# Attention on one core: low parts of the turned weights on GpSimd, and VectorE's scans with an operand in PSUM

## The chip, the cores and the metric

The kernel runs on one core of one Trainium2 chip. The metric is the device time in microseconds of one execution. The engines of the core are TensorE (PE in the profile, with its weight loads as PEld), VectorE (DVE), ScalarE (ACT), GpSimd (POOL) and SyncE (SP), whose queue issues nearly all DMAs. Each engine works through its own instructions in order; semaphores hold an instruction until those that it depends on are done.

## The reference

A decoder trunk of two layers on 1024 positions of width 1024: an RG-LRU block, a feed-forward block, an attention block, a second feed-forward block, and a last norm. The edit lies in the attention, which has 16 heads of 64. In the reference (cut):

```python
z = jnp.einsum("bhqd,bhkd->bhqk", qb, kb).astype(jnp.float32) * scale
strict = s_idx < t_idx
log_fail = jnp.where(strict, jax.nn.log_sigmoid(-z), 0.0)
suffix = lax.cumsum(log_fail, axis=3, reverse=True) - log_fail
weights = jnp.where(strict, jnp.exp(jax.nn.log_sigmoid(z) + suffix), 0.0)
outs.append(jnp.einsum("bhqk,bhkd->bhqd", weights.astype(vb.dtype), vb))
```

Each weight is the chance sigmoid(z) of a position times the product of sigmoid(-z) over the positions between it and the query.

## The kernel before

**How the weights are made.** Let F be sigmoid(-z). The product of F from a position up to the query is what one reversed multiplicative scan along the row gives. The kernel computes these products in place of the weights and moves the difference of neighbouring products onto the values, which are stored as differences of neighbouring rows (L2013). So, for each chunk of 128 queries by up to 512 keys:

- TensorE makes the scores in a PSUM bank (`z_part`, L2091 and L2092, two banks in turn).
- ScalarE writes F = sigmoid of them as float32 into SBUF (`z_rest`, L2129).
- VectorE scans F in place, from right to left (`scan`). A chunk on the diagonal (L2136) multiplies by F and adds `unit`, a row of zeros that ends in a scaled identity block, which starts each row's product at its own diagonal element. A chunk to the left of it (L2139) starts from the first column of the diagonal chunk; its second tensor operand is not used in the arithmetic (`bypass`), and F itself stands there.
- The float32 product is split into two float16 parts in the tile `wx` (four buffers): ScalarE casts the high part (`turn_weights`, L2151) and VectorE subtracts it from F for the low part (L2152).
- One DMA from SyncE's queue (L2161) turns both parts, so that keys lie on the partitions, into `wd`, `wt` or `wp`.
- TensorE multiplies the turned parts by the values (`av_part`, L2203).

In the last of the eight pairs of heads (`q == LAST`) the weights are turned by TensorE instead (`t_part`, L2171) into banks of the pool `psT`, and split from there (`t_split`, L2180 and L2181). `turn_weights` returns at once for that pair. The pool `psT` has two banks, which nothing uses before the last pair.

**The order of work.** Inside `tc.manual_schedule` every engine runs its instructions in the order of the program. Each head has 12 chunks and 12 units of the products with the values. The loop over `u` scores and scans one chunk, splits and turns the chunk of the step before, takes one postponed task from `later`, and issues two steps of `fill`: the projections that make queries, keys and values of the next pair (`qkv_steps`), on TensorE. A chunk's products with the values come about ten steps after its scan. With each chunk of the first seven pairs but the first of a diagonal pair comes a turn, ten for a head, 140 in all: 84 of 512 columns and 56 of 384.

Other work of the stage that shares the queues:

- On VectorE: L1960, low parts of projection weights; L2011 and L2013, values; L2052 and L2066, queries and keys; L2018, low parts of values; L2216, outputs of a head; L2228, low parts of outputs.
- On ScalarE: L1945, squares of weights; L1952, high parts of projection weights; L2041 and L2049, key and query pieces; L2061 and L2074, their casts.
- On GpSimd: L2070, memsets of the unused half of the key tiles `kk`; L1938 to L1941, four small factor instructions; L2220, an addition of values to the output of a pair; L1958, low parts of two weights for the stage that follows.
- On SyncE's queue, beside L2161: L129, loads of weights; L2040 and L2048, copies of key and query pieces to the other half of the partitions; L2022, the turning of the values.

`unit` is made once at the start of the stage by GpSimd (L1896, L1897), in bfloat16. Before the loop, norms are computed by `stats` (square root L205 on ScalarE) and spread over the partitions by TensorE (L216).

Of the kernel before, what the change touches and what calls it, by code (L numbers as in the profile page):

```python
# [8 lines left out]
F32 = mybir.dt.float32  # L9
# [5 lines left out]
ALU = mybir.AluOpType  # L15
# [3 lines left out]
P = 128  # L19
# [4 lines left out]
NB = 512  # L24
# [11 lines left out]
def trunk(  # L36
# [21 lines left out]
    nc = tc.nc  # L58
# [239 lines left out]
    with ExitStack() as st, tc.manual_schedule(engines={E.PE, E.Activation, E.DVE, E.Pool, E.SP}):  # L298
# [95 lines left out]
        for ks in (range(4), range(4, ND)):  # L394
            for lhs, rhs in ((0, xh), (0, xl), (1, xh)):
                for k in ks:
                    first, last = lhs == k == 0 and rhs is xh, lhs == 1 and k == ND - 1
# [1487 lines left out]
    with ExitStack() as st:  # L1885
# [4 lines left out]
        psT = st.enter_context(tc.tile_pool(name="psT", bufs=2, space=PSUM, reuse_waits="tile"))  # L1890
# [4 lines left out]
        unit = ap.tile([P, NB], BF16, name="unit")  # L1895
        nc.gpsimd.memset(unit[:, 0 : NB - P], 0.0)  # L1896
        nc.gpsimd.tensor_scalar_mul(unit[:, NB - P :], ident, UP)  # L1897
        g2 = ap.tile([P, ND], BF16, name="g2")
        nc.scalar.square(g2, vc[:, V_MIX + ND : V_MIX + 2 * ND])
        rs = ap.tile([P, NT], F32, name="rs")  # L1900
# [73 lines left out]
        def qkv_steps(q):  # L1974
            for which in range(3):
                w, at = wq.pop((q, which)), 3 * q + which + 1
                if at < 3 * NP:
                    raw = raws.pop(at)
                    wq[divmod(at, 3)] = next_weights(raw, Q_UP)
                    if which == 1:  # L1980
                        later.extend(column_norms(raw, q))
                else:
                    mix[0].w[mix[0].order[0]] = next_weights(mix[0].raw.pop(0), WO_UP, nc.gpsimd)
                for i in (at + 1,) if at < 3 * NP else (at + 1, at + 2):
                    load_link(i)

                ks = (1, 5, 2, 6, 3, 7, 0, 4) if (q, which) == (0, 0) else range(ND)
                for n in range(NH):
                    pool, tag = (psZ, "z") if (q, which) == (0, 0) else (psQ, "qk")
                    ps = pool.tile([P, NB], F32, tag=tag, name="qk_ps")  # L1990
                    for i, k in enumerate(ks):
                        mm3(ps, w[0][:, k], w[1][:, k], *pair16(xh[k][n]), i == 0, i == ND - 1)
                        if i < ND - 1:
                            yield
                    ev = evacuate(q, which, n, ps)
                    next(ev)
                    yield
                    next(ev, None)
# [102 lines left out]
        LAST = NP - 1  # L2101
# [29 lines left out]
        def scan(q, hx, j, ci, c0, c1, diag):  # L2131
            F = W[q, hx, j, ci]
            n = min(c1, (j + 1) * P) - c0
            rev = F[:, ::-1]
            if diag:
                nc.vector.tensor_tensor_scan(rev, rev, unit[:, NB - n :][:, ::-1], 0.0, op0=ALU.mult, op1=ALU.add)  # L2136
            else:
                first = W[q, hx, j, 1][:, 0:1]
                nc.vector.tensor_tensor_scan(rev, rev, rev, first, op0=ALU.mult, op1=ALU.bypass)  # L2139

        T = {}

        def turn_weights(q, hx, j, ci, c0, c1, diag):
            paired = diag and j % 4 < 2
            if q == LAST or paired and j % 4 == 0:
                return
            F = W[q, hx, j - 1, "pair"] if paired else W[q, hx, j, ci]
            F = F.rearrange("p (b c) -> p b c", c=P)
            m = F.shape[1]
            wx = ap.tile([P, 4, 2, P], F16, tag="wx", name="wx", bufs=4)  # L2150
            nc.scalar.copy(wx[:, 0:m, 0], F)  # L2151
            nc.vector.tensor_sub(wx[:, 0:m, 1], F, wx[:, 0:m, 0])  # L2152
            if paired:
                dst = T[q, hx, j // 4, "pair"] = ap.tile([P, 6, P], F16, tag="wp", name="wp", bufs=2)
            else:
                g = (q, hx, j // 4, diag)
                if g not in T:
                    wide, tag = (2, "wd") if diag else (4, "wt")
                    T[g] = ap.tile([P, 8, wide, P], F16, tag=tag, name=tag, bufs=2)
                dst = T[g][:, 0 : 2 * m, j % 4 - (2 if diag else 0)]  # L2160
            nc.sync.dma_start(dst, wx[:, 0:m].rearrange("p b h c -> p (b h c)"), transpose=True)  # L2161

        def unit_list(q, hx):
            kbs = ((0, 1, 2, 3), (4, 5, 6, 7, 0, 1, 2, 3))
            return [(q, hx, G, kb, kb == 4 * G, kb == 3) for G in range(2) for kb in kbs[G]]
# [70 lines left out]
        units = [u for q, hx in heads for u in unit_list(q, hx)]  # L2236
# [27 lines left out]
        with tc.manual_schedule(engines={E.PE, E.Activation, E.DVE, E.Pool, E.SP}):  # L2264
# [3 lines left out]
            first = qkv_steps(0)  # L2268
# [32 lines left out]
            def turn(some):  # L2301
                for a in some:
                    turn_weights(*a)

            for u in range(-LEAD, len(units)):
# [13 lines left out]
                for a in some:  # L2319
                    scan(*a)  # L2320
# [13 lines left out]
                if u in gains:  # L2334
                    z_rest(z_part(*chunks[c]), *chunks[c])
                    scan(*chunks[c])
                    turning.append(chunks[c])
                    c += 1
# [52 lines left out]
```

## Time and profile before

| what | us |
|---|---|
| median of three runs | 2084.01 |
| lowest and highest of the three | 2081.61 and 2084.85 |
| the profiled execution | 2083.18 |
| its span in the trace | 2081.1 |

Busy time in that execution, by stretches of the span (us from its start): attention proper is the second row, the last pair of heads the third.

| stretch | TensorE | VectorE | ScalarE | GpSimd |
|---|---|---|---|---|
| 940 to 980 | 38.27 | 25.93 | 27.90 | 4.76 |
| 980 to 1340 | 349.19 | 343.48 | 289.97 | 48.90 |
| 1340 to 1385 | 41.08 | 38.97 | 28.59 | 7.56 |

In the rows of a profile, "out<-in" names the tile written and the tiles read, "x" gives the count, and after the bar stand the busy time in us and the mean of one in ns; then, where shown, the idle time of the engine in front of these instructions and what ended it. In rows in order of time, the first number is the start and the second the duration in us; a bracket gives the idle time in front and what ended it. A matmul's row overlaps the next one's, since matmuls are pipelined.

### The profile page before, as it was taken

The page shows a single profiled execution, that of the slowest core. Times are in us where ns is not written, and L with a number is a line of the kernel's source. Part 1 is how long each engine was busy: PE and PEld are TensorE (multiplying, and loading weights), DVE is VectorE, ACT ScalarE, POOL GpSimd, SP SyncE. Part 2 cuts the span into 40 slices and gives each one's busy share as a digit, 9 for nine tenths or more (in the row PEclk, how much of TensorE's full clock was granted, in tenths as well). Part 3 has the DMA queues.
Part 4 walks back from the last instruction along what each step waited for, and adds up shares of the span by engine and source line. Part 5 has one row for each costly group of instructions (what it writes and reads, how often), then busy time and mean ns, then how long its engine had stood idle before and what let it go on. Part 6 is the DMA issues. An engine that isn't in the chain of part 4 may idle for free.

```text
span 2081.1 us, 28578 instructions
## 1 busy us (share of the span) xinstructions
PE 2026.6 (97%) x10059; PEld 1111.7 (53%) x10059; DVE 1847.6 (89%) x2795; ACT 1452.1 (70%) x2279; POOL 116.8 (6%) x154
## 2 busy tenths in 40 slices
PE   8999999999999999999999999999999999999998
PEld 7888885445544444444555555554445545444445
DVE  6887898989898899897999999988899899999886
ACT  6777446777878656566888888755777777665566
POOL 1000010000000000000011111212000000000002
PEclk9999999999999999999999999999999999999999
DMA  7231471675677665233887887754355546674412
GB/s 254 61 97 55 166 222 58 187 231 193 224 228 238 234 219 168 59 101 103 160 157 155 154 153 151 148 175 141 93 195 177 178 153 207 211 257 149 137 46 91
DMA packets 444000, 332.27 MB, mean 160 GB/s; under 512 B 165832, under 2 KB 361552, under 8 KB 443856
## 3 DMA queue, kind: packets, MB, share of 16 engines
q1 hardware_dynamic: 443696, 330.19, 55.0%
q8 instruction: 78, 1.28, 0.3%
q14 instruction: 66, 0.54, 0.1%
q10 hardware_dynamic: 160, 0.27, 0.0%
HBM read 215.55 MB, written 69.21 MB: 137 GB/s over the span
## 4 chain that ended last, share of the span: by engine, by line
PE 59%; DVE 21%; ACT 12%; issue 6%; DMA 2%; SPq 0%; DVEq 0%; ACTq 0%
PE p_ps L158 11%; PE p_ps L156 11%; PE p_ps L157 11%; PE a_ps L157 3%; PE a_ps L158 3%; PE a_ps L156 3%; PE ob_ps L156 2%; PE ob_ps L158 2%; PE ob_ps L157 2%; DVE wx L2152 2%; DVE wa L784 2%; DVE v L1394 2%; ACT kk L2041 1%; ACT w L2129 1%; DVE sb L799 1%
## 5 line engine op out<-in xcount | busy, mean ns | idle before, releaser
L158 PE MATMUL p_ps<-v,wb 128*128 128x512 f16 x524 | 198.8, 379 | 8.1 <-DVE wb L784 7.9
L156 PE MATMUL p_ps<-v,wb 128*128 128x512 f16 x524 | 198.5, 379 | 4.4 <-ACT G L1075 2.6
L158 PE MATMUL p_ps<-v,wc 128*128 128x512 f16 x524 | 198.6, 379 | 3.2 <-DVE wc L784 3.2
L157 PE MATMUL p_ps<-v,wc 128*128 128x512 f16 x524 | 198.6, 379 | 0.0
L157 PE MATMUL p_ps<-v,wb 128*128 128x512 f16 x524 | 198.6, 379 | 0.0
L156 PE MATMUL p_ps<-v,wc 128*128 128x512 f16 x524 | 198.5, 379 | 0.0
L158 PE MATMUL p_ps<-v,wa 128*128 128x512 f16 x396 | 150.1, 379 | 0.0
L157 PE MATMUL p_ps<-v,wa 128*128 128x512 f16 x396 | 150.1, 379 | 0.0
L156 PE MATMUL p_ps<-v,wa 128*128 128x512 f16 x396 | 150.0, 379 | 0.0
L779 ACT ACTIVATE wb<-sb,fac 128x1024 f16<-128x1024 f32 x44 | 50.5, 1148 | 108.8 <-DVE sb L799 108.8
L2151 ACT CAST wx<-w 128x512 f16<-128x512 f32 (+1 forms) x140 | 80.0, 572 | 48.4 <-DVE w L2136 26.4
L156 PE MATMUL p_ps<-v,wd 128*128 128x512 f16 x254 | 96.2, 379 | 6.6 <-ACT G L1486 3.6
L2136 DVE TENSOR_TENSOR_SCAN w<-w,unit 128x128 f32<-128x128 f32 (+1 forms) x112 | 93.4, 834 | 8.8 <-ACT w L2129 7.7
L156 PE MATMUL qk_ps<-rh,w 128*128 128x512 f16 x264 | 101.0, 383 | 0.0
L157 PE MATMUL qk_ps<-rh,w 128*128 128x512 f16 x264 | 100.0, 379 | 0.3 <-DVE rh L250 0.3
L158 PE MATMUL qk_ps<-rh,w 128*128 128x512 f16 x264 | 100.0, 379 | 0.0
L2129 ACT ACTIVATE w<-z_ps,rs 128x512 f32<-128x512 f32 (+2 forms) x168 | 96.4, 577 | 4.6 <-PE z_ps L2092 3.0
L158 PE MATMUL p_ps<-v,wd 128*128 128x512 f16 x254 | 96.3, 379 | 1.5 <-DVE wd L784 1.5
L156 PE MATMUL a_ps<-xh,whi 128*128 128x512 f32 x248 | 97.0, 391 | 0.0
L2091 PE MATMUL z_ps<-kk,q 128*128 128x256 f32 (+1 forms) x192 | 94.1, 490 | 2.9 <-ACT w L2129 1.4
L157 PE MATMUL a_ps<-xl,whi 128*128 128x512 f32 x248 | 96.6, 390 | 0.1
L158 PE MATMUL a_ps<-xh,wlo 128*128 128x512 f32 x248 | 96.6, 389 | 0.0
(489 smaller groups left out, 5591.1 us busy)
## 6 DMA issues: line engine op xcount, KB each, us to landing
raw<-in_ffn_w_in SPq DMA_DIRECT2D x80, 512.0 KB, 4.3
pd<-U SPq DMA_DIRECT2D x90, 256.0 KB, 2.4
loose<-in_ffn_w_out SPq DMA_DIRECT2D x44, 512.0 KB, 4.2
raw<-pd SPq DMA_DIRECT2D x66, 256.0 KB, 3.7
row<-pd SPq DMA_DIRECT2D x62, 256.0 KB, 3.9
raw<-in_ffn_w_out SPq DMA_DIRECT2D x56, 256.0 KB, 3.3
loose<-in_attn_w_qkv SPq DMA_DIRECT2D x24, 512.0 KB, 3.8
raw<-in_attn_w_qkv SPq DMA_DIRECT2D x24, 512.0 KB, 4.6
```

What stands on the lines that cost most here:

```text
L156: nc.tensor.matmul(ps, lhsT=wh, rhs=mh, start=first, stop=False, **kw)
L157: nc.tensor.matmul(ps, lhsT=wh, rhs=ml, start=False, stop=False, **kw)
L158: nc.tensor.matmul(ps, lhsT=wl, rhs=mh, start=False, stop=last, **kw)
L779: nc.scalar.activation(h, r, AF.Copy, scale=up)
L784: V.scalar_tensor_tensor(l, r, up, h, op0=ALU.mult, op1=ALU.subtract)
L799: V.tensor_sub(self.part(self.sb, 0), self.part(self.rb, 0), self.part(self.ra, 0))
L1394: V.scalar_tensor_tensor(lo, raw, power_of(p), hi, op0=ALU.mult, op1=ALU.subtract)
L2091: nc.tensor.matmul(ps[:, 0 : c1 - c0], lhsT=lhsT, rhs=KK[q][hx][:, 0, c0:c1], start=True, stop=False)
L2129: nc.scalar.activation(F, ps[:, 0:n], AF.Sigmoid, scale=rs[:, j : j + 1])
L2136: nc.vector.tensor_tensor_scan(rev, rev, unit[:, NB - n :][:, ::-1], 0.0, op0=ALU.mult, op1=ALU.add)
L2151: nc.scalar.copy(wx[:, 0:m, 0], F)
L2152: nc.vector.tensor_sub(wx[:, 0:m, 1], F, wx[:, 0:m, 0])
```

## The change

The low parts of the turned weights (L2152) are formed by GpSimd. The second tensor operand of the scans in the first seven pairs of heads comes from a PSUM bank, `units_ps`, in which ScalarE writes, once, a reversed float32 copy of `unit`. The bank is the first of the two of `psT`. In the last pair the scans on the diagonal read `unit` in SBUF as before, and those off the diagonal name `unit` in place of F as the operand that is not used.

```diff
         nc.gpsimd.tensor_scalar_mul(unit[:, NB - P :], ident, UP)
+        units_ps = psT.tile([P, NB], F32, tag="T", name="units")
+        nc.scalar.copy(units_ps, unit[:, ::-1])
         g2 = ap.tile([P, ND], BF16, name="g2")
...
             rev = F[:, ::-1]
+            add = unit[:, NB - n :][:, ::-1] if q == LAST else units_ps[:, 0:n]
             if diag:
-                nc.vector.tensor_tensor_scan(rev, rev, unit[:, NB - n :][:, ::-1], 0.0, op0=ALU.mult, op1=ALU.add)
+                nc.vector.tensor_tensor_scan(rev, rev, add, 0.0, op0=ALU.mult, op1=ALU.add)
             else:
                 first = W[q, hx, j, 1][:, 0:1]
-                nc.vector.tensor_tensor_scan(rev, rev, rev, first, op0=ALU.mult, op1=ALU.bypass)
+                nc.vector.tensor_tensor_scan(rev, rev, add, first, op0=ALU.mult, op1=ALU.bypass)
...
             nc.scalar.copy(wx[:, 0:m, 0], F)
-            nc.vector.tensor_sub(wx[:, 0:m, 1], F, wx[:, 0:m, 0])
+            nc.gpsimd.tensor_sub(wx[:, 0:m, 1], F, wx[:, 0:m, 0])
```

## The prediction

> **What bounds the kernel now.** I read the page's engine rows first, then the stage table by stretches of time, then who waits for whom inside the stage that the edit touches, then groups of instructions, then single rows in order of time.
>
> ```profile
> span 2081.1 us, 28578 instructions
> PE 2026.6 (97%) x10059; PEld 1111.7 (53%) x10059; DVE 1847.6 (89%) x2795; ACT 1452.1 (70%) x2279; POOL 116.8 (6%) x154
> ```
>
> Everything edited lies in the attention stage, from about 980 us, when the first chunk is scanned, to 1340 us, when the last head pair, which is not turned by transfers, takes over.
>
> ```profile
> core 0: us, PE busy (x) PEld busy (x) DVE busy (x) ACT busy (x) POOL busy (x), PEclk, DMA share, GB/s
> 980.00:1340.00 360.00, 349.19 (x1864) 187.69 (x1862) 343.48 (x490) 289.97 (x538) 48.90 (x63) 1.00 0.81 156
> ```
>
> In these 360 us VectorE is busy 95%, ScalarE 81%, GpSimd 14%. TensorE's rows leave only 360.00 - 349.19 = 10.8 us idle, at the full clock. So TensorE's own work is the floor, and the change can bring back only what TensorE waits. These are its waits, and those of the engines that make it wait:
>
> ```profile
> ACT wx L2151 <- DVE w L2136: 26.4, 26, 2.4
> ACT wx L2151 <- DVE w L2139: 19.4, 23, 1.8
> PEld z_ps L2091 <- ACT w L2129: 9.5, 18, 0.9
> PE av_ps L2203 <- DMA wt<-wx: 3.6, 5, 1.0
> PE n_ps L1927 <- ACT sq L1945: 3.0, 6, 0.7
> PE z_ps L2091 <- ACT w L2129: 1.4, 7, 0.4
> ...
> SPq L2161 <- DVE wx L2152: 52.6, 45, 3.0
> ```
>
> The third column is the total in us. TensorE waits for three things: for a score bank (L2091) that ScalarE has not read yet, for a turned weight tile (L2203), and for ScalarE's squares (L1927). ScalarE is late because its casts stand in its queue waiting for VectorE's scans, 26.4 + 19.4 = 45.8 us. The transfers are late because SyncE's in-order queue stands at L2161 until VectorE has written the low part, 52.6 us. All three lead back to VectorE. The weight-load wait of 9.5 us lies partly under matmuls already in flight and so is only partly in the 10.8 us of idle time; 10.8 + 9.5 = 20.3 us bounds what can come back.
>
> **The change part by part.** *Subtractions off VectorE.*
>
> ```profile
> L2136 DVE TENSOR_TENSOR_SCAN w<-w,unit 128x128 f32<-128x128 f32 (+1 forms) x112 | 93.4, 834 | 8.8 <-ACT w L2129 7.7
> L2152 DVE TENSOR_TENSOR wx<-w,wx 128x512 f16<-128x512 f32 (+1 forms) x140 | 87.2, 623 | 0.1
> L2139 DVE TENSOR_TENSOR_SCAN w<-w,w 128x512 f32<-128x512 f32 x56 | 75.0, 1339 | 7.3 <-ACT w L2129 7.1
> L1960 DVE SCALAR_TENSOR_TENSOR w<-raw,rx,w 128x512 f16<-128x512 f32 x40 | 29.5, 739 | 0.0
> L2052 DVE TENSOR_TENSOR two<-qk_ps,two 128x512 fp32r<-128x512 f32 x14 | 9.6, 687 | 0.2
> L2052 DVE TENSOR_TENSOR two<-two 128x512 fp32r<-128x512 f32 x14 | 9.6, 683 | 0.0
> L2013 DVE TENSOR_TENSOR t<-vt 128x512 f32<-128x512 f32 x14 | 9.5, 677 | 0.0
> L2018 DVE SCALAR_TENSOR_TENSOR vx<-t,vx 128x512 f16<-128x512 f32 x14 | 9.4, 671 | 0.0
> L2228 DVE SCALAR_TENSOR_TENSOR rl<-oo,av,rl 128x512 f16<-128x512 f32 x7 | 5.2, 736 | 0.0
> L2228 DVE SCALAR_TENSOR_TENSOR xg<-oo,av,xg 128x512 f16<-128x512 f32 x5 | 3.7, 742 | 0.0
> ```
>
> VectorE loses 140 instructions, 87.2 us. Its load falls from 343.5 to 256.3 us before any new contention.
>
> *The same subtractions on GpSimd.* The nearest rows are GpSimd's subtraction with the same three types (L1958: float16 from float32 minus float16, 512 wide) and its float32 addition.
>
> ```profile
> L1958 POOL TENSOR_TENSOR w<-raw,w x4: 1154/2834/3688, 1327.4 to 1368.6; 128x512 f16<-128x512 f32 x4
> L2220 POOL TENSOR_TENSOR oo<-oo,vt x14: 1087/1092/2122, 1032.6 to 1353.9; 128x512 f32<-128x512 f32 x14
> L2070 POOL MEMSET kk<- x16: 944/946/947, 961.9 to 1307.4; 64x1024 f32 x16
> ```
>
> Minimum, median, maximum in ns; the memsets of the keys, which only write, are the longest other work of GpSimd. Between 1.15 and 2.83 us I must choose, and the rows of the slow ones say what made them slow:
>
> ```profile
> 1332.55 3.69 POOL L1958 TENSOR_TENSOR w<-raw,w 128x512 f16<-128x512 f32 x1 [4.00 <-ACT raw L1954]
> ...
> 1333.04 0.66 DVE L2152 TENSOR_TENSOR wx<-w,wx 128x512 f16<-128x512 f32 x1
> 1333.62 0.67 DVE L2013 TENSOR_TENSOR t<-vt 128x512 f32<-128x512 f32 x1
> 1334.22 0.41 DVE L2136 TENSOR_TENSOR_SCAN wp<-wp,unit 128x128 f32<-128x128 f32 x1
> 1334.56 0.65 DVE L2152 TENSOR_TENSOR wx<-w,wx 128x512 f16<-128x512 f32 x1
> 1335.35 1.43 DVE L2136 TENSOR_TENSOR_SCAN wp<-wp,unit 128x256 f32<-128x256 f32 x1
> ```
>
> GpSimd's 3.69 us began while VectorE ran one instruction after another with both inputs in SBUF. VectorE's first gap is at 1335.21; from there to GpSimd's end at 1336.24 are 1.03 us, an undisturbed subtraction. In its turn the scan at 1335.35, twice as wide as the one of 0.41 us, took 1.43 us. So the two exclude each other while VectorE reads two SBUF operands, and a chain of such instructions is not broken into. What happens when one operand is in PSUM:
>
> ```profile
> 1185.78 1.09 POOL L2220 TENSOR_TENSOR oo<-oo,vt 128x512 f32<-128x512 f32 x1 [11.67 <-DVE oo L2216]
> ...
> 1185.73 0.75 DVE L2011 SCALAR_TENSOR_TENSOR vt<-qk_ps,sv,rbc 128x512 f32<-128x512 f32 x1
> 1186.40 1.55 DVE L2136 TENSOR_TENSOR_SCAN w<-w,unit 128x512 f32<-128x512 f32 x1
> ```
>
> L2011 reads a PSUM bank and one SBUF tile. It ran beside the addition, and both took their ordinary time (0.75 and 1.09 us). The scan behind it, with `unit` in SBUF, waited for the addition's end at 1186.87. Scans that take `units_ps` are of L2011's kind, so I take 1.15 us for a 512-wide subtraction (84) and three quarters, 0.87 us, for a 384-wide one (56): 96.6 + 48.7 = 145.3 us. With the 48.9 us it has, GpSimd is busy 194 of 360 us, 54%. The other end, 2.83 us, stays for a rival. [...]
>
> *What remains in contention.* VectorE keeps 94 instructions with two SBUF inputs: L1960, the second group of L2052, L2013, L2018 and L2228 (40 + 14 + 14 + 14 + 12, 67 us together). GpSimd reads SBUF for about 145 us and 14 x 1.09 = 15 us of 360 us, so an instruction meets it with a chance of 0.44 and waits on average half of 1.15 us: 94 x 0.44 x 0.57 = 24 us, put back on VectorE. The ends are 0 and 94 x 1.15 = 108 us. VectorE then stands at 256 + 24 = 280 us (78%); at the bad end 364 us, which would be the bound again, with no gain.
>
> *The PSUM operand's own price.* The two L2052 rows are the same operation with and without a PSUM operand: 687 against 683 ns, 4 ns, so 168 scans pay 0.7 us. L2139 read its own tile as a dummy second operand and now reads the bank; nothing else changes in it. In the last pair both kinds of scan keep an SBUF operand, and cost what they did.
>
> [...]
>
> *Order and waits.* The subtraction no longer waits behind the next scan:
>
> ```profile
> 1197.42 0.62 ACT L2151 CAST wx<-w 128x512 f16<-128x512 f32 x1 [0.26 <-DVE w L2139]
> ...
> 1198.55 1.28 DVE L2139 TENSOR_TENSOR_SCAN w<-w,w 128x512 f32<-128x512 f32 x1
> 1199.74 0.67 DVE L2152 TENSOR_TENSOR wx<-w,wx 128x512 f16<-128x512 f32 x1
> ```
>
> Here cast end to low part took 1200.41 - 1198.04 = 2.37 us; on GpSimd it takes 1.15 when free. The transfer stays in SyncE's queue at its place and now waits for GpSimd; behind it stand the key and query placements (L2040, L2048), the value transfers (L2022) and weight loads (L129), so all move with it. In GpSimd's queue the subtractions join the two key memsets, four small factor instructions and two additions of a pair, all with work of earlier units as input. The longest that can stand in front of a subtraction is the two memsets, 1.9 us. If the subtractions come later than VectorE's did, the four `wx` buffers come free later, and ScalarE's casts wait for a landing.
>
> *The new copy.* ScalarE's copy into `units_ps` needs `unit`, which GpSimd finishes just as ScalarE would go on:
>
> ```profile
> 955.51 0.42 POOL L1896 MEMSET unit<- 128x384 bf16 x1 [89.99 <-DVE rbc L1788]
> 955.89 0.55 POOL L1897 TENSOR_SCALAR unit<-ident 128x128 bf16<-128x128 f32 x1
> ...
> 955.59 0.57 ACT L2061 CAST two<-qk_ps 128x512 fp32r<-128x512 f32 x1
> ...
> 961.63 1.13 PE L216 MATMUL rb_ps<-ident,rcol 128*128 128x128 f32 x8 [0.90 <-DVE rcol L2272]
> ```
>
> ScalarE stands until 956.44, copies for about 0.57, and everything behind is some 1.5 us later. TensorE already waits 0.90 us at L216 for a chain that begins on ScalarE, so I charge 1.5 us in full (ends 0 and 1.6).
>
> *The sum.* Of what is bounded by 20.3 us, the transfer waits (3.6) and the square waits (3.0) go, and half of the score-bank waits, (9.5 + 1.4) / 2 = 5.5: ScalarE at 290 of 360 us is next in line and will still be late at times, after the key pieces above all. 12.1 - 1.5 = 10.6 us. The profiled execution took 2083.18 us (2.1 us outside its span); less 10.6 that is 2072.6. It stood 0.8 us below the median of the three runs, so I predict 2073.
>
> **The rivals.** *No change (0.16).* ScalarE and SyncE's order, not VectorE, set the waits: ScalarE's in-order casts of the keys would hold the squares and the score banks as before. For it: 81% busy. Against: 45.8 us of ScalarE's idle time ends with a scan. Then only the transfer waits go, 3.6 - 1.5 = 2 us: 2082.
>
> *GpSimd's part is late (slower, 0.13).* The wait of L2203 already has no slack: each further lateness of the last off-diagonal tile passes to TensorE, about once in each of seven pairs (five times in the row). If the two memsets (1.9 us) stand before that subtraction, 7 x 1.9 = 13.3 us are added, the 3.6 stay, and against the 8.5 us of the other gains and the 1.5 us of the copy the balance is +6: 2090. It decides from about 1.0 us of lateness. Against it: GpSimd half idle, and the 2.37 us above to live on.
>
> *The port stays contended (slower, 0.05).* If scans still exclude GpSimd, subtractions take the 2.83 us median: 84 x 2.83 + 56 x 2.12 = 356 us, with 48.9 us 405 in a stage of 360: +45, about 2129. The L2011 row speaks against it.
>
> **How the numbers follow.** Forecast 0.66, with its own range 2062 (20.3 us back, and one or two at the end of the stage) to 2079. About 0.2% (4 us) is what can be told from no change. Faster: 0.66 and a little of the first rival, 0.67. Same: 0.15. Slower: 0.13 + 0.05 = 0.18. The range 2060 to 2090 leaves out the contended port and the worse half of the late GpSimd.
>
> **What would show it.** Right: VectorE near 280 of 345 to 350 us in the stage, GpSimd's subtractions with a median near 1.15 us, scans without a stretched maximum, TensorE's waits for `wt` and the squares gone, ScalarE's waits for scans well below 45.8 us. Wrong: a median over 2 us for the subtractions; L2161 waiting for GpSimd longer than 52.6 us; TensorE's `wt` wait grown; or VectorE relieved and the stage still 360 us.

## The result and the profile after

| | median us | runs | lowest to highest |
|---|---|---|---|
| before | 2082.81 | 4 | 2081.22 to 2084.85 |
| changed | 2066.61 | 4 | 2065.59 to 2067.92 |

The ratio is 0.9923, with a 95% interval of 0.9909 to 0.9936: 16.2 us faster. The prediction forecast 2073 us, 10.6 us less than the profiled execution. Profile against profile it is 16.4 us (2083.18 to 2066.78).

The page of the changed kernel, span and engine rows:

```profile
span 2063.8 us, 28621 instructions
PE 2020.5 (98%) x10059; PEld 1112.3 (54%) x10059; DVE 1787.1 (87%) x2655; ACT 1454.0 (70%) x2280; POOL 260.8 (13%) x294
```

To see where the time came from, I cut both traces at the same instruction, the first scaling of the keys in a pair of heads (L2066 before, L2068 after). The second of these and the one of five pairs later stand at 1057.16 and 1312.69 us before, at 1053.02 and 1295.95 after. The busy times of the engines between them, in the order of the stage table shown earlier, first of the kernel before:

```profile
core 0: us, PE busy (x) PEld busy (x) DVE busy (x) ACT busy (x) POOL busy (x), PEclk, DMA share, GB/s
1057.16:1312.69 255.53, 246.95 (x1318) 132.22 (x1317) 245.74 (x351) 205.16 (x381) 32.82 (x45) 1.00 0.81 155
```

and of the changed kernel, with the stage and its end below:

```profile
1053.02:1295.95 242.93, 242.93 (x1321) 133.10 (x1320) 202.53 (x252) 206.49 (x381) 134.78 (x146) 1.00 0.88 164
...
980.00:1328.00 348.00, 346.47 (x1876) 189.72 (x1875) 289.88 (x356) 294.36 (x542) 193.49 (x204) 1.00 0.87 163
1328.00:1370.00 42.00, 39.64 (x231) 23.79 (x230) 35.63 (x53) 26.32 (x51) 7.44 (x3) 1.00 0.32 107
```

Five pairs took 255.53 us and now take 242.93: 51.11 and 48.59 us a pair. Of the 17.3 us by which the span is shorter, 4.1 are there at the first cut, 12.6 come in these five pairs, 0.6 after them. TensorE now works for the whole of the stretch, 242.93 of 242.93 us. Before, it was idle for only 255.53 - 246.95 = 8.6 us of it, yet 12.6 came back. The other 4.0 us lay inside its busy time: matmul rows overlap their neighbours while the stream runs (in the kernel before, rows of 0.38 us start at 1163.31, 1163.53 and 1163.74 us), and the same matmuls (1318 and 1321 records) covered 246.95 us in a broken stream and 242.93 in an unbroken one. The prediction's bound, idle time plus the weight loads' waits for score banks, allowed for this; idle time alone would not have.

The waits of the changed kernel from 980 to 1328 us (total us, times, longest):

```profile
POOL wx L2155 <- ACT wx L2154: 131.2, 103, 18.2
DVE w L2139 <- ACT w L2131: 31.0, 51, 1.6
ACT w L2131 <- PE z_ps L2094: 26.8, 47, 1.2
DVE w L2142 <- ACT w L2131: 22.9, 33, 2.5
...
ACT wx L2154 <- DVE w L2139: 6.7, 13, 1.0
...
ACT wx L2154 <- DVE w L2142: 4.6, 7, 1.2
...
PEld z_ps L2093 <- ACT wd L2131: 1.7, 3, 0.8
...
PE z_ps L2093 <- ACT wd L2131: 0.9, 2, 0.7
PEld z_ps L2093 <- ACT w L2131: 0.8, 2, 0.4
...
PEld L2206 <- DMA wt<-wx: 0.2, 1, 0.2
...
SPq L2164 <- POOL wx L2155: 56.5, 66, 2.3
```

The direction has turned round. ScalarE waited 45.8 us for scans in the prediction's stage and waits 11.3; VectorE waits 31.0 + 22.9 us for sigmoids, and ScalarE 26.8 us for scores. TensorE's wait for a turned tile is gone but for 0.2 us, its wait for the squares is gone, and of its waits for score banks 3.4 us are left. Only 0.8 us of these are waits for the `w` tiles, which the prediction counted with 10.9; the other 2.6 us, for `wd`, belong to the start of the last pair, which waited 2.9 us for them before (980 to 1345 us). The new instructions and the scans (minimum, median, maximum in ns):

```profile
L2155 POOL TENSOR_TENSOR wx<-w,wx x140: 909/1158/3303, 982.9 to 1318.0; 128x512 f16<-128x512 f32 x84, 128x384 f16<-128x384 f32 x56
...
L2139 DVE TENSOR_TENSOR_SCAN w<-w,units x112: 404/812/1221, 979.9 to 1304.5; 128x128 f32<-128x128 f32 x28, 128x256 f32<-128x256 f32 x28, 128x384 f32<-128x384 f32 x28, 128x512 f32<-128x512 f32 x28
L2142 DVE TENSOR_TENSOR_SCAN w<-w,w,units x56: 1253/1279/1281, 993.0 to 1315.2; 128x512 f32<-128x512 f32 x56
```

No scan of the first seven pairs is stretched any more. Of what VectorE still runs with two operands in SBUF, these groups count (from 980 to 1328 us; L2231, not shown, is at 750 ns and was at 736):

```profile
L1962 DVE SCALAR_TENSOR_TENSOR w<-raw,rx,w 128x512 f16<-128x512 f32 x40 | 35.8, 895 | 0.0
...
L2054 DVE TENSOR_TENSOR two<-two 128x512 fp32r<-128x512 f32 x14 | 16.8, 1199 | 0.0
L2015 DVE TENSOR_TENSOR t<-vt 128x512 f32<-128x512 f32 x15 | 13.3, 887 | 0.0
...
L2020 DVE SCALAR_TENSOR_TENSOR vx<-t,vx 128x512 f16<-128x512 f32 x14 | 10.4, 740 | 0.0
```

Against the means of before (739, 683, 677, 671 ns) that is 40 x 156 + 14 x 516 + 15 x 210 + 14 x 69 ns = 17.6 us of contention with GpSimd. The recorded texts call what the two engines contend for a port; the rows show when the two exclude each other, not what they share.

### The profile page after: what moved, and what is told of

Read it like the earlier page. It is cut to its first block, busy times and chain, and to the rows that moved or that the text cites. A ratio compares the mean times of both kernels' runs of the same rounds, so it can differ in the third digit from the quotient of the medians.

```text
span 2063.8 us, 28621 instructions
## 1 busy us (share of the span) xinstructions
PE 2020.5 (98%) x10059; PEld 1112.3 (54%) x10059; DVE 1787.1 (87%) x2655; ACT 1454.0 (70%) x2280; POOL 260.8 (13%) x294
## 4 chain that ended last, share of the span: by engine, by line
PE 71%; DVE 15%; ACT 8%; issue 3%; DMA 2%; POOL 0%; SPq 0%; DVEq 0%; ACTq 0%; POOLq 0%
PE p_ps L158 11%; PE p_ps L156 11%; PE p_ps L157 11%; PE qk_ps L156 4%; PE qk_ps L158 4%; PE qk_ps L157 4%; PE a_ps L157 3%; PE a_ps L158 3%; PE a_ps L156 3%; PE av_ps L2206 3%; PE ob_ps L156 2%; PE ob_ps L158 2%; PE ob_ps L157 2%; DVE v L1394 2%; PE z_ps L2093 2%
## 5 line engine op out<-in xcount | busy, mean ns | idle before, releaser
L2155 POOL TENSOR_TENSOR wx<-w,wx 128x512 f16<-128x512 f32 (+1 forms) x140 | 157.9, 1128 | 163.7 <-ACT wx L2154 131.2
L2139 DVE TENSOR_TENSOR_SCAN w<-w,units 128x128 f32<-128x128 f32 (+1 forms) x112 | 91.4, 816 | 32.1 <-ACT w L2131 31.0
L2131 ACT ACTIVATE w<-z_ps,rs 128x512 f32<-128x512 f32 (+2 forms) x168 | 97.2, 579 | 29.4 <-PE z_ps L2094 26.8
L244 POOL TENSOR_TENSOR acc<-acc,rbc 128x512 f32<-128x512 f32 x30 | 40.8, 1360 | 493.9 <-ACT rbc L243 493.8
```

The costliest lines, as they stand in the source:

```text
L244: (eng or nc.gpsimd).tensor_add(acc[n], acc[n], sq)
L2131: nc.scalar.activation(F, ps[:, 0:n], AF.Sigmoid, scale=rs[:, j : j + 1])
L2139: nc.vector.tensor_tensor_scan(rev, rev, add, 0.0, op0=ALU.mult, op1=ALU.add)
L2155: nc.gpsimd.tensor_sub(wx[:, 0:m, 1], F, wx[:, 0:m, 0])
```

## The experiments

The theory: VectorE paced each pair of heads, and what it lost in work came back until TensorE was the floor. Rivals: the low part's earlier arrival did it; the PSUM operand alone did it; ScalarE or SyncE set the pace. All times below are medians, each kernel with its own ratio to the kernel before on the same chip; the stretch is that of the five pairs as above.

| kernel | median us | ratio, 95% | stretch | TensorE busy | VectorE busy, idle | GpSimd busy |
|---|---|---|---|---|---|---|
| before | 2082.81 | | 255.53 | 246.95 | 245.74, 9.79 | 32.82 |
| changed | 2066.61 | 0.9923 (0.9909 to 0.9936) | 242.93 | 242.93 | 202.53, 40.40 | 134.78 |
| subtraction alone | 2094.41 | 1.0054 (1.0039 to 1.0069) | 264.14 | 249.19 | 241.68, 22.46 | 181.04 |
| scans alone | 2074.85 | 0.9961 (0.9948 to 0.9974) | 248.17 | 246.04 | 238.81, 9.36 | 25.59 |
| off-diagonal scans as before | 2074.31 | 0.9963 (0.9950 to 0.9976) | 248.77 | 245.66 | 218.60, 30.17 | 158.85 |
| idle work, half width | 2068.46 | 0.9929 (0.9912 to 0.9945) | 242.93 | 242.93 | 223.70, 19.23 | 134.84 |
| idle work, full width | 2078.19 | 0.9981 (0.9972 to 0.9990) | 249.70 | 246.20 | 240.36, 9.34 | 138.36 |
| no low part | 2066.14 | 0.9918 (0.9903 to 0.9933) | 242.93 | 242.93 | 190.86, 52.07 | 72.21 |
| a fifth on GpSimd | 2069.72 | 0.9944 (0.9928 to 0.9961) | 244.13 | 243.96 | 228.81, 15.32 | 50.27 |
| off-diagonal ones twice | 2091.05 | 1.0049 (1.0032 to 1.0066) | 261.82 | 248.20 | 209.86, 51.96 | 196.52 |
| turn ahead of scan | 2117.26 | 1.0169 (1.0153 to 1.0184) | 277.28 | 253.24 | 250.26, 27.02 | 34.09 |

**Each half alone.** First the subtraction moved, with the scans as before:

```diff
-            nc.vector.tensor_sub(wx[:, 0:m, 1], F, wx[:, 0:m, 0])
+            nc.gpsimd.tensor_sub(wx[:, 0:m, 1], F, wx[:, 0:m, 0])
```

> The subtractions go to GpSimd, the scans keep their second operand in SBUF. Theory (two SBUF operands on VectorE exclude GpSimd): VectorE's two-operand work of about 235 us (scans 168, the rest 67) and GpSimd's reading of about 160 us exclude each other, 395 us in a stage of 360; subtraction median well over 2 us, stage 385 to 400 us, 2110 to 2130 us in all. Rival (the relief of VectorE alone does it, the PSUM operand does not matter): subtraction median 1.16 us and about 2067 us.

It was slower than before by 0.54%, some 11 us: the sign that the theory of exclusion wants, at less than the price expected. Its subtractions, one of VectorE's groups, and TensorE's waits for a score bank:

```profile
L2152 POOL TENSOR_TENSOR wx<-w,wx x140: 911/1544/3937, 983.2 to 1348.8; 128x512 f16<-128x512 f32 x84, 128x384 f16<-128x384 f32 x56
...
L1960 DVE SCALAR_TENSOR_TENSOR w<-raw,rx,w 128x512 f16<-128x512 f32 x39 | 48.2, 1236 | 0.0
...
PEld z_ps L2091 <- ACT w L2129: 23.2, 30, 1.6
...
PE z_ps L2091 <- ACT w L2129: 11.2, 18, 1.1
```

The median subtraction is 1.54 us, not the 2.83 us of the four rows that the prediction took for its worst rival. Still both engines lose: L1960 takes 1236 instead of 739 ns, and VectorE, rid of 100 instructions in the five pairs, is hardly less busy there (241.68 us, 245.74 before). Then the scans alone, with the subtraction on VectorE:

```diff
-            nc.gpsimd.tensor_sub(wx[:, 0:m, 1], F, wx[:, 0:m, 0])
+            nc.vector.tensor_sub(wx[:, 0:m, 1], F, wx[:, 0:m, 0])
```

> The scans take their operand from PSUM, the subtractions stay on VectorE. Theory: VectorE's load stays near 340 of 360 us, TensorE's waits for banks, squares and turned tiles stay; 2080 to 2083 us (some 5 us of stretched scans less on VectorE, 0.8 us lost at the new copy). Rival (the scans are what became faster): near 2067 us.

It brought 0.39%, some 8 us, about half of the whole change, where I had expected nearly nothing. The scans of the kernel before:

```profile
L2136 DVE TENSOR_TENSOR_SCAN w<-w,unit x112: 405/816/1558, 980.1 to 1321.1; 128x128 f32<-128x128 f32 x28, 128x256 f32<-128x256 f32 x28, 128x384 f32<-128x384 f32 x28, 128x512 f32<-128x512 f32 x28
...
L2139 DVE TENSOR_TENSOR_SCAN w<-w,w x56: 1264/1280/2220, 993.5 to 1331.8; 128x512 f32<-128x512 f32 x56
```

Those of this kernel, and its stretch of five pairs:

```profile
L2139 DVE TENSOR_TENSOR_SCAN w<-w,units x112: 401/812/1217, 979.4 to 1311.6; 128x128 f32<-128x128 f32 x28, 128x256 f32<-128x256 f32 x28, 128x384 f32<-128x384 f32 x28, 128x512 f32<-128x512 f32 x28
L2142 DVE TENSOR_TENSOR_SCAN w<-w,w,units x56: 1260/1276/1281, 992.8 to 1322.3; 128x512 f32<-128x512 f32 x56
...
1055.02:1303.19 248.17, 246.04 (x1325) 133.05 (x1324) 238.81 (x351) 205.01 (x381) 25.59 (x45) 1.00 0.83 160
```

The medians are what they were; the maxima fell from 1558 and 2220 ns to 1217 and 1281. So the small work that GpSimd always had stretched a few scans, and that was enough: the scans' rows in the five pairs sum to 115.9 us in place of 121.4, VectorE's busy time fell by 6.9 us and the stretch by 7.4. The two halves do not add: +11 and -8 make +3, the whole is -16. The subtraction is worth moving only once the scans take an operand from PSUM.

**Does an operand that is not used count?** In the changed kernel the off-diagonal scans name F in SBUF again, which the arithmetic ignores (`bypass`):

```diff
-                nc.vector.tensor_tensor_scan(rev, rev, add, first, op0=ALU.mult, op1=ALU.bypass)
+                nc.vector.tensor_tensor_scan(rev, rev, rev, first, op0=ALU.mult, op1=ALU.bypass)
```

> The change, with the off-diagonal scans naming F in SBUF as their unused operand, as before the change; the diagonal ones keep the bank. Port theory: 71 us of scans exclude GpSimd again, in place of the 166 us of e1_sub_only; the subtractions' median lies between 1.16 and 1.54 us and the time between the change's 2067 and e1's 2094 us: 2070 to 2082 us. Rival (an operand that is not used in the arithmetic is not read, or does not hold the port): 2065 to 2069 us, scans' maximum 1.28 us.

```profile
L2142 DVE TENSOR_TENSOR_SCAN w<-w,w x56: 1251/1283/2176, 993.5 to 1322.0; 128x512 f32<-128x512 f32 x56
```

It counts. These 56 scans reach 2176 ns, GpSimd is busy 158.85 instead of 134.78 us, and 2074.3 us gives back half of the gain. VectorE is not overloaded by that (218.60 us busy of 248.77); single scans come late, and ScalarE's casts and TensorE's score banks behind them:

```profile
ACT wx L2154 <- DVE w L2142: 16.2, 14, 1.9
...
PEld z_ps L2093 <- ACT w L2131: 6.1, 7, 1.2
```

**Putting the load back.** If VectorE's load made the time, idle work on VectorE must give it back though the low parts still come early. The changed kernel got, behind each subtraction, an addition into a tile that nothing reads, with one operand in PSUM (GpSimd was busy 134.84 us of the five pairs beside them, 134.78 without them):

```diff
+        idle = ap.tile([P, 2 * P], F16, name="idle")
...
+            nc.vector.tensor_add(idle[:, 0 : m * 64], units_ps[:, 0 : m * 64], unit[:, 0 : m * 64])
```

> The change, and 140 further additions on VectorE, each behind the place of a subtraction and half as wide, reading units_ps and unit into an idle tile: some 0.42 us each at 256 columns and 0.35 at 192, 55 us together, so that VectorE's load is about 290 + 55 = 345 us, as before the change, while the low parts still come from GpSimd and the additions cannot exclude GpSimd. Theory (VectorE's load): most of the gain is lost, 2078 to 2086 us. Rival (the low parts come earlier, the load does not matter): within 3 us of the change, 2064 to 2070 us.

This miss taught most: 140 additions of 0.37 us, and the time hardly moved (2068.5, where 2078 to 2086 was expected). But VectorE was busy only 223.70 of 242.93 us. A load theory needs a threshold, and the same additions at full width (`m * P`, tile of `NB`) were to pass it:

> As e3_load_back, with the further additions as wide as the subtractions (0.68 and 0.53 us, 87 us in all). Theory, now with a threshold: a pair of heads takes TensorE's 48.6 us, or VectorE's work of the pair and some 2.2 us in which it waits for sigmoids, whichever is more. VectorE's work of a pair was 48.7 us before the change, 47.5 in e2_scan_only and 44.5 in e3_load_back; with e3's 7.4 us of additions replaced by 12.5 it is about 49.5, the pair takes 51.7 us, seven pairs lose 22 us against the change: 2083 to 2092 us. Rival (the early low parts count, not the load): within 3 us of the change.

```profile
1056.42:1306.12 249.70, 246.20 (x1325) 132.95 (x1325) 240.36 (x352) 205.84 (x381) 138.36 (x146) 1.00 0.84 159
...
L2157 DVE TENSOR_TENSOR idle<-units,unit 128x512 f16<-128x512 f32 (+1 forms) x139 | 84.7, 609 | 0.0
...
ACT wx L2155 <- DVE w L2140: 21.4, 26, 2.0
```

They did: 2078.2 us, 11.6 slower than the changed kernel, and ScalarE waits for scans again. It is less than expected: contention shrank at the same time (L2055, which is L2054 of the changed kernel, is back at 684 ns, from 1199). The table now reads as one rule. In the three kernels that VectorE paces (before, scans alone, full-width idle work) it is idle for 9.79, 9.36 and 9.34 us of the stretch, 1.9 us a pair under each of these loads, and the stretch is its busy time plus that. Where busy time plus 9.4 stays below 242.93 (223.70, 202.53, 190.86 busy) the stretch is TensorE's 242.93 to the hundredth. (The kernel with a fifth on GpSimd, below, is an exception of 1.2 us. Subtraction alone, off-diagonal scans as before, the doubled subtraction and the turn ahead of the scan lie outside the rule: there VectorE is idle 22 us and more, and something comes late.) The earlier low part, which the full-width kernel kept, did not make the gain.

**Nothing beyond the floor.** The next kernel leaves the low parts of the weights out (zeros in their place):

```diff
-            nc.gpsimd.tensor_sub(wx[:, 0:m, 1], F, wx[:, 0:m, 0])
+            nc.gpsimd.memset(wx[:, 0:m, 1], 0.0)
```

> The change with GpSimd's subtraction replaced by a memset of zero of the same part, which only writes: the low parts of the weights are left out. Theory (TensorE's own pace is now the floor): no more than 2 us below the change, 2064 to 2067 us, although VectorE's stretched instructions (L1962, L2054, L2015) return to their ordinary times. Rival (contention with GpSimd still costs): 2055 to 2061 us.

GpSimd's work is nearly halved (72.21 us in the five pairs, 134.78 in the changed kernel), VectorE is freed of contention (L1962 at 724 ns, L2054 at 681, L2015 at 670), and the time is 2066.1 against 2066.6, the stretch 242.93 again. In these five pairs only less work for TensorE could bring more.

**How much must go?** Four of a pair's twenty subtractions on GpSimd:

```diff
-            nc.gpsimd.tensor_sub(wx[:, 0:m, 1], F, wx[:, 0:m, 0])
+            (nc.gpsimd if hx == 0 and not diag else nc.vector).tensor_sub(wx[:, 0:m, 1], F, wx[:, 0:m, 0])
```

> The change, with GpSimd forming only the low parts of one head's off-diagonal chunks of each pair, 4 of 20; VectorE forms the other 16. Theory with the threshold: VectorE's work of a pair is 47.5 - 4 x 0.685 + some 0.5 of new contention = 45.2 us, with 2.2 us still under TensorE's 48.6, so nearly the whole gain: 2065 to 2069 us. Rival (gain in proportion to the subtractions moved): a fifth of the way from e2_scan_only's 2075 to the change's 2067, 2072 to 2075 us.

2069.7 us, just above the range expected, and a stretch of 244.13. Much of that gain is the scans' part, which alone gives a ratio of 0.9961 and a stretch of 248.17. From there the fifth brings the stretch 4.0 of the 5.2 us down to the floor; of the whole time it brings about half of what is left (0.9944, on the way to 0.9923), with intervals nearly as wide as that difference. VectorE stands at 228.81 + 9.4 = 238.2, 4.7 us under the floor, and yet the stretch is 1.2 us above it: from 980 to 1328 us ScalarE still waits 18.0 + 17.9 us for scans, and TensorE 3.5 + 0.2 us for score banks of `w` tiles. So the rule is not sharp just below the floor.

**How much slack has GpSimd?** Each off-diagonal subtraction is done twice on GpSimd:

```diff
+            if not diag:
+                nc.gpsimd.tensor_sub(wx[:, 0:m, 1], F, wx[:, 0:m, 0])
```

> The change, with GpSimd forming the low part of each off-diagonal chunk twice over, so that their transfers start some 1.15 us later and GpSimd is busy 45 us more. The prediction held that the turned off-diagonal tile has no slack: then TensorE's wait for wt comes back, about 1.15 us a pair, seven pairs, 8 us more than the change: 2073 to 2077 us. The threshold theory holds that the slack is there as long as VectorE does not pace the pair: 2065 to 2069 us, TensorE's wait for wt under 2 us.

```profile
DVE w L2142 <- POOL wx L2157: 8.5, 5, 1.7
...
ACT wx L2154 <- DMA wp<-wx: 13.6, 10, 3.4
ACT wx L2154 <- DMA wt<-wx: 8.8, 5, 1.8
PE av_ps L2208 <- DMA wt<-wx: 8.6, 10, 1.2
...
SPq L2166 <- POOL wx L2155: 113.8, 85, 5.1
```

2091 us, slower than before, and far outside what I expected. GpSimd is busy 196.52 of 261.82 us, three quarters, which looked like room. But chunks are off the diagonal four steps in a row; there a turn of 2 x 1.16 us meets steps of 48.59 / 24 = 2.0 us, GpSimd falls behind within the run (SyncE's queue waits up to 5.1 us for one subtraction, 2.3 in the changed kernel; one of L2155 took 3.74 us, where the median is 1.16), and SyncE's queue, ScalarE's casts (which wait for a landing) and TensorE follow. This is the prediction's rival of a late GpSimd, real, and not met by one subtraction a chunk.

**Two smaller questions.** Latency was to be tested in the kernel before, by issuing the turn ahead of the next scan:

```diff
+                now, turning = turning, list(some)
+                turn(now)
                 for a in some:
                     scan(*a)
-                now, turning = turning, list(some)
-                turn(now)
```

> The kernel before with one edit: VectorE subtracts the low part of the last chunk ahead of this chunk's scan, where it stood behind it. The low part and its transfer come a scan (about 1.2 us) earlier, VectorE's load is the same. Theory (load): within 4 us of the kernel before, 2080 to 2088 us. Rival (latency of the low part): a good part of the gain, 2068 to 2076 us.

```profile
DVE wx L2152 <- ACT wx L2151: 33.6, 42, 2.0
```

2117 us, outside both ranges: VectorE now stands before a subtraction until ScalarE has cast, with a ready scan behind it. The test says nothing on latency; it shows that the order in VectorE's queue was itself worth some 35 us. Last, the copy into PSUM was moved out of the start of the stage (step 30 of a table of work done once):

```diff
-        nc.scalar.copy(units_ps, unit[:, ::-1])
...
+                30: lambda: nc.scalar.copy(units_ps, unit[:, ::-1]),
```

> The change, with ScalarE's copy into units_ps issued at step 30 of the first projections, where ScalarE waits anyway, in place of the start of the stage. TensorE's wait at L216 should fall from 1.70 to about 0.90 us: about 0.8 us less than the change, 2064 to 2067 us. Rival (the copy cost nothing there): the same as the change, and the wait at L216 stays.

TensorE's wait at L216, in the changed kernel and in this one:

```profile
961.41 1.13 PE L216 MATMUL rb_ps<-ident,rcol 128*128 128x128 f32 x8 [1.70 <-DVE rcol L2275]
```

```profile
962.07 1.13 PE L216 MATMUL rb_ps<-ident,rcol 128*128 128x128 f32 x8 [0.89 <-DVE rcol L2274]
```

The copy costs 0.8 us there, as the wait shows; the total (2066.43, ratio 0.9924, 0.9909 to 0.9939) cannot tell it apart. No kernel tried beats the changed one by a measurable margin.

## Why the prediction was right, and where it was not

**Held.** VectorE was the pacing engine, and the load put back shows it. The exclusion showed in both directions: subtractions at a median of 1158 ns (140 in 157.9 us, 145.3 forecast), unstretched scans beside them (at most 1221 and 1281 ns), and the loss when the scans stay in SBUF (2094 us). The PSUM operand cost the scans nothing that shows: 812 against 816 ns and 1279 against 1280 in the medians. Contention was 17.6 us (24 forecast). The transfer and square waits went.

**Mis-sized, the score banks.** The sum credited half of their waits, 5.5 us, because ScalarE "is next in line". It was not: it is as busy as before (206.49 us in the five pairs, 205.16 before) and TensorE now runs there without a break. ScalarE had been late only behind the scans. Of the 10.9 us of these waits 0.8 are left, so 10.1 went, nearly twice the credit. With the transfers' 3.6, the squares' 3.0 and the copy's 0.8 against them that makes 15.9 of 16.2 us. That it comes so close is in part luck, for a weight load's wait can lie under running matmuls (before, one of 0.29 us that ended at 1164.13 lay under two matmul rows, from 1163.74 to 1164.34), and waits that the prediction did not list went too. Two of them, from 980 to 1328 us in the kernel before:

```profile
PEld L1927 <- ACT sq L1945: 3.7, 7, 0.8
...
PE av_ps L2203 <- issue: 1.4, 1, 1.4
```

The first of these makes 20.3 us no strict bound. How much of each wait lay under running matmuls no view tells, so the account fits, and no more than that is shown.

**Left out, the old stretching of scans.** The prediction quoted a scan of 1.43 us, held up by GpSimd, and then costed the PSUM operand at 0.7 us without crediting what it saves. By itself that half of the change was worth 8 us.

**Wrong step, right outcome: VectorE's load.** 343.5 - 87.2 + 24 gave 280 us; it is 289.9, with less contention than assumed. Rows of neighbouring instructions overlap. Over the five pairs, all groups of VectorE sum to 270.3 us before and 215.6 after, while its busy time is 245.74 and 202.53: the rows lost 54.7 us, the engine 43.2. Subtracting full rows from a busy time takes away too much. Neither this step nor the stretched scans enter the sum, which adds up TensorE's waits alone: the forecast's range was not spoiled by them, and its coming true does not bear them out.

**Not needed, the earlier low part.** The 2.37 us shortened to about 1.16 were not what gained. And the marker "L2161 waiting for GpSimd longer than 52.6 us" misled: it waits 56.5 us, and TensorE waits only 0.2 us for a transfer. The sum of a queue's waits does not tell whether the last of them matters. Nor were the memsets the longest work in front of a subtraction, as the prediction read them: SyncE's queue stands at L2164 for up to 1.9 us (15.8 in all) behind the additions L2223, and for up to 1.6 us (8.1 in all) behind the memsets.

**The copy** cost 0.8 us, not 1.5: ScalarE took L2063's cast first, and only 0.3 us of its wait for `unit` was left.

**The rivals.** No change: excluded, for ScalarE and SyncE's order did not set the waits. GpSimd late: not in this kernel, but the doubled subtraction shows it at the place named. Contended port: not here, but with SBUF scans it happens, at 2094 and not 2129 us, since four slow rows beside back-to-back VectorE work had been taken for all 140.

## What to carry to other kernels

Find the engine that paces a stage by its busy time plus the wait that it cannot lose (here 9.4 us in five pairs), and expect a gain of one for one only until the next engine's floor; beyond it nothing more came (6.9 us of VectorE's busy time brought 7.4 us of the stretch with the scans alone; with the low parts left out the stretch stayed at 242.93), and a part of the move may bring most of it. Before work goes to GpSimd, take one input of VectorE's long instructions out of SBUF (2066.6 us with that here, 2094.4 without), and look at the tightest run of steps, not at GpSimd's share of busy time (2091 us at three quarters). Bound a gain on TensorE by its weight-load waits too, and do not subtract whole rows from a busy time when they overlap.

## What was not expected of the hardware

- An operand that a scan names and does not use (`bypass`) still counts as one in SBUF: off-diagonal scans of up to 2176 ns with it in SBUF, 1281 with it in PSUM, and GpSimd busy 158.85 us of five pairs instead of 134.78.
- GpSimd's light work of before (32.82 us in 255.53) cost up to 7.4 us of that stretch, mostly through stretched scans.
- Back-to-back VectorE instructions overlap in the trace by (270.3 - 245.74) / 351 = 0.07 us each.
- Two things stay open: why VectorE waits 1.9 us a pair even where it is the bound, and what a shorter way from scan to transfer is worth by itself.
